# A transformer layer's opening, the start of its ConvFFN and the down projection's operands rearranged

## The chip, the cores and the metric

The kernel runs on one core of a Trainium2 chip, in one launch. The metric is the device time of the whole launch in microseconds. The core has five engines that work side by side and wait for each other through semaphores: TensorE (matrix products, into PSUM banks), VectorE, ScalarE, GpSimd (elementwise work; GpSimd doesn't touch PSUM) and SyncE, whose queue issues all of this kernel's DMAs.

## The reference

One layer of a diffusion backbone on 1024 tokens of width 1024, with 256 context tokens, all float32:

```
mod_x = silu(c) @ w_ada + b_ada              # six vectors: shift, scale, gate, twice
hx = rms_norm(x) * (1 + sc1) + sh1           # the context likewise, with its own c
...                                          # Fourier branch and gated DeltaNet branch on hx
x = x + gt1 * rms_norm(merged @ w_out)
h = rms_norm(x) * (1 + sc2) + sh2
a, u = split(h @ w_up)                       # two halves of 2816 channels
a = dwconv2d(a, conv_ffn)                    # 3x3 on the 16 x 64 grid of tokens
x = x + gt2 * rms_norm((silu(a) * u) @ w_down)
```

## The kernel before, in words

**Products in three parts.** Matrix products are made at float32's precision from faster float32r products: each operand is split into a high part (a copy to float32r) and a low part (the operand less the high part), and high x high, high x low and low x high are summed in a PSUM bank. So every operand costs one copy and one difference on ScalarE, VectorE or GpSimd. `halves` and `weights` load and split a weight tile, `split` an activation; a weight's low part overwrites its raw tile.

**The order of instructions.** The function `layer` records operations in a natural order. `Program.schedule` then orders them for each engine: it gives each operation a cost by a formula, ranks it by the longest path to the end plus a `bonus` that the code sets around urgent parts, and hands out ready operations by rank in a simulated time. What it decides is fixed in the program; on the chip each engine goes through its list in order. Tiles live in pools, stacked from the left or the right of SBUF; a tile that reuses the words of another, of its own ring or of a pool closed before, waits for the other's last reader. A PSUM bank is named by a tag ("X0", "Y0", "X1", "Y1", "pp", "pf", "pd", "pm"), one 128x512 tile each.

**The opening** (from `rows`, and `hidden_x`). The first 2048 columns of `w_ada`, shift and scale, are loaded in 16 tiles of 128x1024 (row block k, `half` 0 for the shift and 1 for the scale), split, and multiplied with `s4`, which holds the high and the low part of silu(c) for the tokens and the context in four columns. The four rows of 512 are then transposed and summed into `mod`. `hidden_x` normalizes x, transposes it in blocks of 512 tokens, applies `mod` on ScalarE and splits the result: the high part on VectorE, the low part on VectorE and GpSimd in turn. `decays` is the first product behind it.

**The output projection** (loop `for ts in ...`). For each tile of 128 tokens, 48 matmuls (`wo_group`: 8 row blocks k of the weights, three part products, two banks), then `post` (norm over the two banks and residual; squares on ScalarE, a power on GpSimd, the rest on VectorE), a store of the new residual to DRAM, a second norm, and scaling in place. Tokens 6 and 7 are done together. After four tiles (g = 0, and again g = 1) `transposed` and ScalarE make `hh[k, g]`, the modulated hidden tile, channel block k by 512 tokens.

**The ConvFFN.** The up projection is one level of a Strassen scheme: instead of eight products of half matrices there are seven per column block c of 128 channels (22 blocks). The right operands `RB[m]` are four tiles each, made once: `side_b` splits an `hh` tile, `sum_b` first adds or subtracts two. RB[1] and RB[3] need the first 512 tokens alone, RB[4] the second, RB[0], RB[2], RB[5] and RB[6] both. For each c, `both` loads four raw weight tiles; `summed` makes sums of them on GpSimd, `split_w` splits on ScalarE and GpSimd; `chain` is 12 matmuls into bank A, B or C. A block has seven chains, 84 matmuls, called here by the code's names m1 to m7, recorded as 2, 5, 1, 4, 3, 7, 6; between chains of one bank its result is evicted (to `v_`, `u_` or the padded grid `apad`). The 3x3 convolution follows: per half one ScalarE and eight VectorE operations in PSUM, then silu and the product with u, and a store to DRAM (`gdr`).

**The down projection.** Three groups of token tiles (3, 3 and 2); for each, the 22 blocks of the gated activation are loaded back, split (`down_g`, low part on GpSimd) and multiplied with `w_down`'s split blocks, most of which stay in SBUF.

## Time and profile before

| | |
|---|---|
| median of 3 runs | 2068.61 us (2061.31 to 2069.54) |
| the profiled execution | 2066.87 us |
| its span, first to last instruction | 2065.2 us |
| mean granted TensorE clock | 0.973 |
| TensorE, weight loads, VectorE, ScalarE, GpSimd busy | 94%, 76%, 65%, 41%, 32% |
| DMA | 257.5 MB, mean 125 GB/s |

The profile is one execution. Its page gives each engine's busy time, a map of 40 slices (each digit the busy share in tenths; PEclk the granted TensorE clock in tenths), the chain of work that ended last, and groups of instructions with count, busy time, mean duration and the idle time before them by what ended it. All operations are recorded by one helper, so every row has its line (L349); one tells them apart by engine, operation, operands (m is an SBUF tile, p a PSUM bank, d a DRAM tile), shape and time. PE is TensorE, PEld its weight loads, DVE VectorE, ACT ScalarE, POOL GpSimd, SPq the DMA queue. Besides the page, the answers for one stretch are used: busy times by stretch, the timeline of one engine, and the groups of a stretch.

### The profile page before, as it was taken

What the parts mean: (1) busy time and instruction counts of PE and PEld (TensorE: products, weight loads), DVE (VectorE), ACT (ScalarE), POOL (GpSimd) and SP (SyncE); (2) the same over time, 40 slices, a digit from 0 to 9 for tenths busy, and PEclk for the clock granted to TensorE, in tenths of its full rate; (3) what the DMA queues carried; (4) which work ended last, traced back from release to release, by engine and by line L of the source; (5) the groups of instructions that cost most, each with busy time, mean ns of one, the idle gap of its engine ahead of it and who ended that gap; (6) DMA issues with size and microseconds to landing.
All of it is one profiled execution on the core that took longest, in us unless ns stands there. A gap on an engine that the chain in (4) does not pass through costs nothing. (4 is left out here: it accounts for less than half of the span.)

```text
span 2065.2 us, 31554 instructions
## 1 busy us (share of the span) xinstructions
PE 1949.2 (94%) x11470; PEld 1573.0 (76%) x11470; DVE 1349.2 (65%) x2780; ACT 856.5 (41%) x2074; POOL 670.9 (32%) x671
## 2 busy tenths in 40 slices
PE   6988999899998999999999999949999999999998
PEld 2777878687787788778787778728788888887886
DVE  7647776768677677673756484477988888891021
ACT  6367345555354453533431132334444444541121
POOL 4210121201112220210211000387888888722222
PEclk9999999899998999999999999959999999999999
DMA  7143324344442543341778462302222222452231
GB/s 285 44 163 120 105 85 138 113 137 134 119 135 53 154 151 100 111 114 46 226 251 306 162 214 96 113 33 69 90 82 81 84 83 81 158 201 88 86 124 53
DMA packets 180637, 257.52 MB, mean 125 GB/s; under 512 B 75921, under 2 KB 97522, under 8 KB 180482
## 3 DMA queue, kind: packets, MB, share of 16 engines
q1 hardware_dynamic: 180482, 255.51, 38.6%
q8 instruction: 90, 1.47, 0.3%
q14 instruction: 65, 0.53, 0.1%
HBM read 194.52 MB, written 60.94 MB: 124 GB/s over the span
## 5 line engine op out<-in xcount | busy, mean ns | idle before, releaser
L349 PE MATMUL p<-m,m 128*128 128x512 f32 (+7 forms) x11310 | 1934.7, 338 | 98.5 <-ACT m L349 51.8
L349 PEld LDWEIGHTS p<-m,m 128*128 128x128 f32 (+4 forms) x11310 | 1554.1, 174 | 469.7 <-ACT m L349 77.3
L349 POOL TENSOR_TENSOR m<-m,m 128x512 fp32r<-128x512 f32 (+7 forms) x436 | 556.8, 1297 | 713.1 <-DVE m L349 382.9
L349 ACT ACTIVATE m<-m 128x512 fp32r<-128x512 f32 (+9 forms) x635 | 407.8, 656 | 623.7 <-DMA m<-d 152.0
L349 DVE TENSOR_TENSOR m<-m,m 128x512 f32<-128x512 f32 (+26 forms) x1006 | 528.2, 536 | 112.9 <-ACT m L349 87.3
L349 ACT ACTIVATE m<-p 128x512 f32<-128x512 f32 (+5 forms) x510 | 221.8, 447 | 325.5 <-PE p L349 283.1
L349 DVE SCALAR_TENSOR_TENSOR m<-p,m,m 128x128 f32<-128x128 f32 (+4 forms) x488 | 202.9, 451 | 89.9 <-ACT m L349 40.1
L349 DVE SCALAR_TENSOR_TENSOR p<-m,m,p 128x512 f32<-128x512 f32 x352 | 240.2, 750 | 3.0
L349 ACT ACTIVATE m<-p,m 128x128 f32<-128x128 f32 (+2 forms) x240 | 115.4, 491 | 194.8 <-PE p L349 181.5
L349 POOL MEMSET m<- 128x1024 f32 (+7 forms) x79 | 35.1, 456 | 369.3 <-PE p L349 223.6
L349 DVE SCALAR_TENSOR_TENSOR m<-m 128x1 f32<-128x1 f32 (+1 forms) x25 | 5.0, 199 | 197.3 <-ACT m L349 197.3
L349 POOL COPY m<-m 32x256 f32<-32x256 f32 (+2 forms) x136 | 60.6, 449 | 205.7 <-DMA m<-d 172.6
L349 DVE TENSOR_TENSOR m<-p,m 128x512 f32<-128x512 f32 (+4 forms) x91 | 57.9, 647 | 55.7 <-PE p L349 53.0
L349 DVE SCALAR_TENSOR_TENSOR m<-m,m 128x512 f32<-128x512 f32 (+5 forms) x119 | 66.7, 568 | 33.6 <-ACT m L349 21.2
L349 DVE COPY m<-p 32x256 f32<-32x256 f32 (+10 forms) x116 | 42.2, 368 | 65.3 <-PE p L349 34.6
L349 DVE TENSOR_TENSOR m<-m,p 128x128 f32<-128x128 f32 (+3 forms) x117 | 53.4, 459 | 28.3 <-PE p L349 27.1
L349 DVE SCALAR_TENSOR_TENSOR m<-m,m,m 128x1024 f32<-128x1024 f32 (+2 forms) x68 | 54.4, 801 | 19.3 <-DMA m<-in_w_ada_dram 18.8
L349 ACT ACTIVATE p<-p 128x128 f32<-128x128 f32 x208 | 55.0, 265 | 19.3 <-PE p L349 17.3
L349 DVE SCALAR_TENSOR_TENSOR m<-m,p 128x512 f32<-128x512 f32 x76 | 50.8, 682 | 15.4 <-PE p L349 10.6
L349 DVE SCALAR_TENSOR_TENSOR m<-m,m,p 128x128 f32<-128x128 f32 x128 | 42.7, 342 | 23.1 <-PE p L349 22.5
L349 ACT ACTIVATE m<-m,m 128x128 f32<-128x128 f32 (+1 forms) x168 | 54.5, 400 | 6.2 <-DMA m<-d 5.0
L349 POOL TENSOR_SCALAR_AFFINE_SELECT m<-m 128x1024 f32<-128x1024 f32 x16 | 18.8, 1191 | 100.1 <-DVE m L349 100.1
(20 smaller groups left out, 227.3 us busy)
## 6 DMA issues: line engine op xcount, KB each, us to landing
m<-d SPq DMA_DIRECT2D x76, 512.0 KB
d<-m SPq DMA_DIRECT2D x138, 256.0 KB
m<-d SPq DMA_DIRECT2D x114, 256.0 KB
m<-in_wi_dram SPq DMA_DIRECT2D x106, 256.0 KB
m<-in_w_ada_dram SPq DMA_DIRECT2D x48, 512.0 KB
m<-in_wu_dram SPq DMA_DIRECT2D x88, 256.0 KB
m<-in_wn_dram SPq DMA_DIRECT2D x26, 512.0 KB
m<-d SPq DMA_DIRECT2D x44, 192.0 KB
```

What stands on the lines that cost most here:

```text
L349: return getattr(engine.real, method)(*[real(v) for v in args], **{k_: real(v) for k_, v in kw.items()})
```

## The change

*Opening.* The shift half of `w_ada` is no longer split: eight tiles `whole`, multiplied as plain float32 with `s`, into rows of two; the scale half is split as before, its low parts on VectorE and GpSimd in turn. The modulated token tile takes three tags in turn instead of one. In `hidden_x` the high part goes to VectorE and ScalarE in turn, the low part always to VectorE. The weights of `decays` get tiles of their own.

*Start of the ConvFFN.* The tiles of the split output weights are laid out in pairs, k by k. Three pairs of banks take turns in the output projection; its last group is tokens 5, 6, 7: five row blocks for all three, then the last three for each. All sums and low parts of RB move to VectorE, all high parts to ScalarE. The tiles for u and v come ahead of RB's, which are 22; the last of RB[5] takes a free tile of two older pools. The seven chains of blocks 0 and 1 are recorded interleaved, those that need only the first tokens first; the convolution becomes a function of its own. The first tokens' `hh` and most evictions get a bonus.

*Down projection.* The low parts of the activation move from GpSimd to VectorE.

```diff
-WB = {"H": 8, "L": 8, "h": 3, "l": 3, "fh": 2, "fl": 3, "woh": 8, "wol": 8, "dh": 3, "dl": 3}
+WB = {"H": 8, "L": 8, "h": 3, "l": 3, "fh": 2, "fl": 3, "woh": 8, "wol": 8, "dh": 3, "dl": 3, "LT": 2, "tk": 2}
...
-    rows = [ps(t_, [4, HALF], f"modr{i}") for i, t_ in enumerate(("pd", "pm", "pp", FBANK))]
+    rows = [ps(t_, [(2, 4)[i // 2], HALF], f"modr{i}") for i, t_ in enumerate(("pd", "pm", "pp", FBANK))]
...
     for k in range(KT):
-        for half in range(2):
+        whole = hx.tile([P, D], F32, tag="LH"[k % 2], name=f"w_ada{k}0", bufs=KT)
+        sp.dma_start(whole, a["w_ada"][k * P:(k + 1) * P, 0:D])
+        for j in range(2):
+            te.matmul(rows[j], s[:, k, :], whole[:, j * HALF:(j + 1) * HALF], start=k == 0, stop=k == KT - 1)
+        for half in range(1, 2):
             parts = halves(a["w_ada"][k * P:(k + 1) * P, half * 1024:(half + 1) * 1024], hx, ("H", "L"),
-                           f"ada{k}{half}", (ve, po)[half * (k % 2)])
+                           f"ada{k}{half}", (ve, po)[k % 2])
             for j in range(2):
                 for i, w_ in enumerate(parts):
                     te.matmul(rows[half * 2 + j], s4[:, k, :], w_[:, j * HALF:(j + 1) * HALF], start=k + i == 0,
...
-        mr = dt("th", f"modrow{q}", (4, HALF))
+        n = (2, 4)[q // 2]
+        mr = dt("th", f"modrow{q}", (n, HALF))
         ve.tensor_copy(mr, rows[q])
         for j in range(4):
-            te.transpose(pm_[:, q * 4 + j, :], mr[:, j * P:(j + 1) * P], ident[0:4, 0:4])
+            te.transpose(pm_[:, q * 4 + j, 0:n], mr[:, j * P:(j + 1) * P], ident[0:n, 0:n])
...
-    ve.tensor_tensor(mod, mod, pm_[:, :, 2:4], op=ALU.add)
+    ve.tensor_tensor(mod[:, 8:16, :], mod[:, 8:16, :], pm_[:, 8:16, 2:4], op=ALU.add)
...
-                xt = dt("th", f"xm{k}{g}", (P, HALF))
+                xt = dt(("N", "N", "th")[k % 3], f"xm{k}{g}", (P, HALF))
                 se.activation(xt, pt, AF.Identity, scale=mod[:, 8 + k, 0:1], bias=mod[:, k, 0:1])
-                split(hH[k][:, hs], hL[k][:, hs], xt, ve, (ve, po)[k % 2])
...
-        wba = weights(a["wi"][0], "ba")
+        wba = weights(a["wi"][0], "ba", tags=("LT", "tk"), pl=dp)
...
     wop = pool("wo", bufs=1, side="right")
+    for _ in range(KT):
+        for t_ in ("woh", "wol"):
+            wop.tags.setdefault(t_, []).append(wop.region(D))
...
-        (ve.tensor_copy(h_, src) if n % 2 else se.activation(h_, src, AF.Copy))
-        (ve, po)[n % 2].tensor_tensor(l_, src, h_.bitcast(F32), op=ALU.subtract)
...
-        (ve, po)[(m + n) % 2].tensor_tensor(t_, x_, y_, op=op)
+        ve.tensor_tensor(t_, x_, y_, op=op)
...
-    wo_banks = [("X0", "Y0"), ("X1", "Y1")] * 3 + [("X0", "Y0"), ("pp", FBANK)]
+    wo_banks = [("X0", "Y0"), ("X1", "Y1"), ("pp", FBANK), ("X0", "Y0"), ("X1", "Y1"), ("pp", FBANK), ("X0", "Y0"),
+                ("X1", "Y1")]
...
-    for ts in ((0,), (1,), (2,), (3,), (4,), (5,), (6, 7)):
+    for ts in ((0,), (1,), (2,), (3,), (4,), (5, 6, 7)):
         pts, xts = {}, {}
+        early = 5 if len(ts) > 1 else 0
         for t in ts:
             xts[t] = wp.tile([P, D], F32, tag="xt", name=f"xr{t}", bufs=5)
             sp.dma_start(xts[t], a["x"][t * P:(t + 1) * P, :])
             pts[t] = [ps(wo_banks[t][g], [P, HALF], f"wo{t}{g}") for g in range(2)]
-        for k in range(KT):
+        for k in range(early):
             for t in ts:
                 wo_group(t, k, pts[t], 3 * k)
         for t in ts:
+            for k in range(early, KT):
+                wo_group(t, k, pts[t], 3 * k)
             xt = xts[t]
             post(pts[t], xt, g1r, f"o{t}", wp)
...
         g = ts[-1] // 4
+        prog.bonus = BON * (1 - g)
         for k in (0, 4, 1, 5, 2, 6, 3, 7) if g == 0 else (4, 5, 6, 7, 0, 1, 2, 3):
             pt = transposed(xn[-4:], k, f"h2{g}", ("pd", "pm")[k % 2])
...
+        prog.bonus = 0.0
...
     RAW, WH, WL = 8, 5, 5
-    h2p = pool("h2p", bufs=24, side="right")
+    upr = pool("upr", bufs=1, side="right")
+    for t_, n, m in (("v", 2, HALF), ("u", 3, T)):
+        upr.tags[t_] = [upr.region(m) for _ in range(n)]
+    h2p = pool("h2p", bufs=22, side="right")
...
     for i in range(4):
+        if i == 3:
+            rings[5] = (mp[0], mp[1])
         sum_b(5, hh[i, 0], hh[i, 1], ALU.add, i)
     close(hb)
-    upr = pool("upr", bufs=1, side="right")
...
+        def step(m):
+            if m == 2:
+                chain(A, summed("u0", "u1", ALU.add, "m2"), 1, True)
+                first(lambda: se.activation(v_, A, AF.Copy, scale=-1.0))
+            elif m == 5:
+                chain(B, summed("a0", "a1", ALU.add, "m5"), 4, True)
...
+                chain(A, split_w(raw["u1"], f"m4{c}", True), 3, False)
+                first(lambda: se.activation(u_[:, 0:HALF], A, AF.Copy))
...
+
+        def first(f):
+            prog.bonus = BON
+            f()
+            prog.bonus = 0.0
+
+        def last():
+            conv(c, ap_, inner, u_)
+        return step, last
...
+    pairs = [both(c) for c in range(2)]
+    for m, c in ((2, 0), (4, 0), (2, 1), (4, 1), (5, 0), (5, 1), (3, 0), (3, 1), (1, 0), (7, 0), (6, 0), (1, 1), (7, 1),
+                 (6, 1)):
+        pairs[c][0](m)
+        if m == 6:
+            pairs[c][1]()
+    for c in range(2, NC_FF):
+        step, last = both(c)
+        for m in (2, 5, 1, 4, 3, 7, 6):
+            step(m)
+        last()
+    for p_ in (h2p, upr, wq, lp[1], lp[0], mp[1], mp[0], upl):
         close(p_)
...
             gl = gst.over(gf, F32R, f"gl{c}_{blk}")[:, 0:width]
-            po.tensor_tensor(gl, gf, gh.bitcast(F32), op=ALU.subtract)
+            ve.tensor_tensor(gl, gf, gh.bitcast(F32), op=ALU.subtract)
```

The steps not shown (m = 1, 3, 5 and 7) wrap their chain and eviction in the same way; the evictions behind m7 and m6 have no bonus.

More of the change, by code (lines that the diff above doesn't have):

```diff
@@ L655, in hidden_x @@
                 pt = transposed(xs, k, f"x{g}", XY[k % 4])
-                xt = dt("th", f"xm{k}{g}", (P, HALF))
+                xt = dt(("N", "N", "th")[k % 3], f"xm{k}{g}", (P, HALF))
                 se.activation(xt, pt, AF.Identity, scale=mod[:, 8 + k, 0:1], bias=mod[:, k, 0:1])
-                split(hH[k][:, hs], hL[k][:, hs], xt, ve, (ve, po)[k % 2])
+                split(hH[k][:, hs], hL[k][:, hs], xt, (ve, se)[k % 2], ve)
     def hc(k):
@@ L1470, in side_b @@
         h_, l_ = m_tile(hp, f"bH{m}{n}"), m_tile(lp_, f"bL{m}{n}")
-        (ve.tensor_copy(h_, src) if n % 2 else se.activation(h_, src, AF.Copy))
-        (ve, po)[n % 2].tensor_tensor(l_, src, h_.bitcast(F32), op=ALU.subtract)
+        se.activation(h_, src, AF.Copy)
+        ve.tensor_tensor(l_, src, h_.bitcast(F32), op=ALU.subtract)
         RB.setdefault(m, []).append((h_, l_))
@@ L1584, in both, with conv @@
         grid = lambda t_: t_.rearrange("p (a b) -> p a b", b=GW)
-        chain(A, summed("u0", "u1", ALU.add, "m2"), 1, True)
-        se.activation(v_, A, AF.Copy, scale=-1.0)
-        chain(B, summed("a0", "a1", ALU.add, "m5"), 4, True)
-        ve.tensor_tensor(v_, v_, B, op=ALU.subtract)
-        chain(C, summed("a0", "u1", ALU.add, "m1"), 0, True)
-        ve.tensor_tensor(v_, v_, C, op=ALU.add)
-        chain(A, split_w(raw["u1"], f"m4{c}", True), 3, False)
-        se.activation(u_[:, 0:HALF], A, AF.Copy)
-        chain(B, split_w(raw["a0"], f"m3{c}", True), 2, False)
-        se.activation(inner(1), grid(B), AF.Copy)
-        chain(A, summed("a1", "u1", ALU.subtract, "m7"), 6, False)
-        ve.tensor_tensor(inner(0), grid(A), grid(v_), op=ALU.add)
-        chain(B, summed("u0", "a0", ALU.subtract, "m6"), 5, False)
-        ve.tensor_tensor(u_[:, HALF:T], B, v_, op=ALU.add)
+        def step(m):
[4 more added lines that the diff above has]
+                chain(B, summed("a0", "a1", ALU.add, "m5"), 4, True)
+                first(lambda: ve.tensor_tensor(v_, v_, B, op=ALU.subtract))
+            elif m == 1:
+                chain(C, summed("a0", "u1", ALU.add, "m1"), 0, True)
+                first(lambda: ve.tensor_tensor(v_, v_, C, op=ALU.add))
+            elif m == 4:
+                chain(A, split_w(raw["u1"], f"m4{c}", True), 3, False)
+                first(lambda: se.activation(u_[:, 0:HALF], A, AF.Copy))
+            elif m == 3:
+                chain(B, split_w(raw["a0"], f"m3{c}", True), 2, False)
+                first(lambda: se.activation(inner(1), grid(B), AF.Copy))
+            elif m == 7:
+                chain(A, summed("a1", "u1", ALU.subtract, "m7"), 6, False)
+                ve.tensor_tensor(inner(0), grid(A), grid(v_), op=ALU.add)
+            else:
+                chain(B, summed("u0", "a0", ALU.subtract, "m6"), 5, False)
+                ve.tensor_tensor(u_[:, HALF:T], B, v_, op=ALU.add)
+        def first(f):
[5 more added lines that the diff above has]
+        return step, last
+    def conv(c, ap_, inner, u_):
         for g in range(2):
@@ L1613, in both @@
             sp.dma_start(gdr[c, :, hs], th_)
-    for c in range(NC_FF):
-        both(c)
-    for p_ in (upr, h2p, wq, lp[1], lp[0], mp[1], mp[0], upl):
+    pairs = [both(c) for c in range(2)]
[10 more added lines that the diff above has]
+    for p_ in (h2p, upr, wq, lp[1], lp[0], mp[1], mp[0], upl):
         close(p_)
```

## The prediction

> **What bounds the kernel now.** I read the page's busy table and its forty slices first, then the busy times by stretch, then the engines' timelines around the two places that stand out.
>
> ```profile
> span 2065.2 us, 31554 instructions
> PE 1949.2 (94%) x11470; PEld 1573.0 (76%) x11470; DVE 1349.2 (65%) x2780; ACT 856.5 (41%) x2074; POOL 670.9 (32%) x671
> PE   6988999899998999999999999949999999999998
> PEclk9999999899998999999999999959999999999999
> ```
>
> TensorE bounds it: 94% busy, and every slice but a few is full. What a change can take away is TensorE's idle and half-clock time. There are two such places that the diff touches: the opening (first slices) and the valley of slice 27 between the output projection and the ConvFFN. Rows by stretch, columns: length, then PE, PEld, DVE, ACT, POOL busy, the granted clock, DMA share and GB/s.
>
> ```profile
> 29.00:39.50 10.50, 8.04 (x32) 2.91 (x30) 8.34 (x11) 6.37 (x10) 3.51 (x3) 0.72 1.03 407
> 43.00:58.60 15.60, 9.88 (x50) 6.64 (x48) 14.23 (x34) 13.08 (x24) 9.84 (x8) 0.83 0.00 1
> 1338.30:1391.80 53.50, 22.88 (x69) 14.03 (x69) 40.68 (x41) 19.03 (x33) 43.47 (x35) 0.62 0.09 32
> 1391.80:1396.00 4.20, 4.20 (x11) 3.33 (x12) 1.34 (x2) 0.00 (x0) 2.00 (x2) 0.56 0.00 0
> 1396.00:1427.00 31.00, 31.00 (x139) 25.63 (x138) 21.29 (x31) 14.14 (x23) 23.35 (x18) 1.00 0.19 58
> 1600.00:1700.00 100.00, 100.00 (x443) 82.84 (x442) 88.41 (x126) 43.59 (x74) 81.01 (x63) 1.00 0.24 82
> 1820.00:1840.00 20.00, 20.00 (x87) 16.01 (x86) 20.00 (x25) 8.02 (x12) 6.62 (x6) 1.00 0.37 124
> 1860.00:1900.00 40.00, 40.00 (x172) 32.04 (x171) 2.77 (x5) 6.26 (x15) 8.68 (x9) 1.00 0.15 43
> ```
>
> In the valley TensorE is busy 22.9 of 53.5 us, at 0.62 of its clock: about 14 us of work at full clock, so some 39 us are lost, and 2 more in the half-clock run-up behind it (4.2 us at 0.56). VectorE (40.7) and GpSimd (43.5) are the busy ones there. Before and behind it TensorE is full; in the down projection (1860 on) it is full with VectorE nearly idle.
>
> **The valley, now.** TensorE's timeline (start, length, engine, operation, count, idle before and releaser):
>
> ```profile
> 1329.67 7.20 PE L349 MATMUL p<-m,m 128*128 128x512 f32 x32
> 1337.53 0.73 PE L349 MATMUL p<-m,m 128*128 128x512 f32 x2 [0.66 <-ACT m L349]
> 1366.50 2.06 PE L349 MATMUL p<-m,m 128*128 128x512 f32 x3 [5.31 <-ACT m L349]
> 1387.50 1.22 PE L349 MATMUL p<-m,m 128*128 128x512 f32 x2 [9.81 <-ACT m L349]
> ```
>
> The output projection ends at 1336.9; call it W. The seven chains of column blocks 0 and 1 are 168 matmuls. Of the 69 instructions in the valley 32 are transposes of the second token half, 37 are chain matmuls; 11 follow by 1396; the other 120 run at 31.0/139 = 0.22 us (a few records may be missing) and end at 1422.4. So blocks 0 and 1 are through at W+85.5. I price the new valley as the time from W to that point.
>
> **The valley, changed.** Without any wait: 168 x 0.22 = 37.0, plus the 32 transposes (groups of the valley, the last three of the whole run; columns: count, busy us, mean ns, idle before and releasers):
>
> ```profile
> L349 PE MATMUL p<-m,m 128*128 128x128 f32 x32 | 7.6, 387 | 8.6 <-DVE m L349 5.5 <-ACT m L349 3.1
> L349 DVE TENSOR_TENSOR m<-m,m 128x512 f32<-128x512 f32 x11 | 15.8, 1443 | 2.0 <-POOL m L349 1.2 <-ACT m L349 0.5
> L349 DVE TENSOR_TENSOR m<-m,m 128x512 fp32r<-128x512 f32 x11 | 11.9, 1080 | 4.7 <-ACT m L349 4.7
> L349 DVE CAST m<-m 128x512 fp32r<-128x512 f32 x11 | 8.6, 782 | 4.9 <-ACT m L349 2.5 <-POOL m L349 2.3
> ...
> L349 ACT ACTIVATE m<-m 128x512 fp32r<-128x512 f32 x330 | 205.7, 628 | 379.7 <-POOL m L349 138.5 <-DVE m L349 77.8 <-PE p L349 67.9
> L349 ACT ACTIVATE m<-p,m 128x512 f32<-128x512 f32 x80 | 56.4, 719 | 94.1 <-PE p L349 82.2 <-DVE m L349 8.3 <-POOL m L349 3.4
> L349 DVE TENSOR_TENSOR m<-p,m 128x512 f32<-128x512 f32 x80 | 54.5, 686 | 55.7 <-PE p L349 53.0 <-ACT m L349 2.5
> ```
>
> 7.6 x 0.62 = 4.7 us at full clock. The floor is 41.7, and with two waits for an eviction between chains of one bank (about 1 us each) W+44. Step by step:
>
> Chains 2 and 4 of both blocks need only the first token half. The ordering by hand puts them first, and the output weights now lie k by k, so that the ConvFFN's raw weights fall on k = 0, 1 and their split parts on k = 2 to 4, which the last group (three token tiles, five k's first) finishes 54 matmuls, 11.9 us, before W. Of GpSimd's 24 sums and differences for the two blocks the eight for the first five chains then fit ahead of W+1, and four more follow as chains give up their buffers. The third tile of that group takes the banks that tile 4 has just left; its first product may wait for tile 4's norm, but the other tiles' products stand ready: nothing (0 to 2). So TensorE does four chains, 10.6 us plus the two waits, to W+12.6, where it now waits.
>
> The last token tile must pass its norm meanwhile. For tile 4, with engines free, that took from the first square to the end of the scaling:
>
> ```profile
> 1316.02 0.60 ACT L349 ACTIVATE m<-p 128x512 f32<-128x512 f32 x1 [5.22 <-PE p L349]
> 1323.91 0.76 DVE L349 TENSOR_SCALAR m<-m,m 128x1024 f32<-128x1024 f32 x1 [2.16 <-DMA d<-m]
> 1319.46 1.28 DVE L349 TENSOR_TENSOR m<-m,m 128x512 f32<-128x512 f32 x2
> 1360.25 2.92 DVE L349 TENSOR_TENSOR m<-m,m 128x512 fp32r<-128x512 f32 x2 [0.47 <-ACT m L349]
> 1332.65 14.29 POOL L349 TENSOR_TENSOR m<-m,m 128x512 f32<-128x512 f32 x11 [0.40 <-PE p L349]
> 1391.62 1.09 POOL L349 TENSOR_TENSOR m<-m,m 128x512 fp32r<-128x512 f32 x1 [1.14 <-DVE m L349]
> ```
>
> 8.7 us; I take W+9.5. Tiles 5 and 6 end 8 and 4 us before W now and are hidden. Then come the operands from the second half: 4 differences and 16 sums with 16 differences, all on VectorE: 36 operations. Alone VectorE takes 0.64 (1319.46), beside a busy GpSimd 1.46 (1360.25) or, by the two groups above, (15.8 + 11.9)/22 = 1.26. The two take turns, so I add both: 36 x 0.64 = 23.0, GpSimd's remaining 12 operations for the blocks at 1.09 = 13.1, three for block 2 = 3.3, and 3 of the 5.5 us of VectorE's eight evictions (0.69) that I guess don't overlap: 42.4, so the last operand stands at W+52. The 11 casts (8.6 us) go to ScalarE, which has 20 copies at 0.63 and 8 evictions at 0.72 there: 18 us, hidden behind VectorE's. Chains 5, 3, 1 and 7 are done by then; the last, chain 6 of block 1, ends 3.5 us later: **W+55.5**, a gain of 30. The Trainium skill, page "SBUF — State Buffer", section "Who interferes with whom", says that a VectorE operation with two SBUF inputs and a reading GpSimd one exclude each other for a whole instruction, and the loser waits. By that rule the sum is the one just made from the rows; the plain mean of 1.26 is the rival below.
>
> Costs of the same edit: the convolutions of blocks 0 and 1 queue behind that VectorE work. VectorE has 88.4 of 100 us in the steady stage, so it wins back 2 us a block of 18.5 us (84 x 0.22); I take 2 us of TensorE waits (0 to 8). The last operand tile of chain 6 now lies where the down projection's second weight block is loaded, so that load waits for the ConvFFN's very last chain: 1 us (0 to 4), since the first weight block covers 18 x 0.22 = 4 us. Raising evictions in rank: nothing (-1 to 3), TensorE being full there.
>
> **The opening.** Now:
>
> ```profile
> L349 PE MATMUL p<-m,m 128*4 128x512 f32 x64 | 20.9, 478 | 14.5 <-ACT m L349 9.2 <-DVE m L349 5.2
> L349 PE MATMUL p<-m,m 128*1 128x512 f32 x16 | 8.2, 590 | 0.0
> L349 POOL TENSOR_TENSOR m<-m,m 128x1024 fp32r<-128x1024 f32 x8 | 20.0, 2504 | 78.7 <-DVE m L349 39.7 <-PE p L349 14.0 <-DMA m<-in_wo_dram 12.6
> 6.28 1.06 ACT L349 ACTIVATE m<-m 128x1024 fp32r<-128x1024 f32 x1 [3.64 <-DMA m<-in_w_ada_dram]
> 28.64 2.27 ACT L349 ACTIVATE m<-m 128x1024 fp32r<-128x1024 f32 x2 [0.22 <-DMA m<-in_w_ada_dram]
> 34.93 1.20 DVE L349 TENSOR_TENSOR m<-m,m 128x1024 fp32r<-128x1024 f32 x1
> 33.30 6.13 PE L349 MATMUL p<-m,m 128*4 128x512 f32 x22 [2.17 <-DVE m L349]
> 42.50 0.24 DVE L349 SCALAR_TENSOR_TENSOR m<-m,m 128x8 f32<-128x8 f32 x2
> ```
>
> The last modulation weights are in by 30.9, but a late low part (to 36.1) holds the products to 39.4, and the modulation is ready at 42.7. Changed, half of the weights need no split: ScalarE loses 8 and VectorE 8 of the 1024-wide operations. The last low part is GpSimd's (2.5 us, behind a copy that ends near 30): done near 32.5. TensorE's load grows: a plain product is two instructions of 8.2/16 = 0.51 us, 32 of them 16.4, plus 32 split ones at 20.9/64 = 0.33, 10.5: 27 us from the first landing near 6.3, so about 34. That is 5.4 before today. Behind it VectorE gives up 8 casts and takes 8 differences of the main tokens, about even; the decay weights in tiles of their own and four buffers more for the modulated tokens only let work start earlier, nothing to 1. I take **5 us**; 9 if the products keep up with the landings, -8 if half of the 27 us run at half clock (13 us more).
>
> **The down projection.** TensorE enters it without a gap:
>
> ```profile
> 1797.79 32.40 PE L349 MATMUL p<-m,m 128*128 128x512 f32 x138 [0.71 <-POOL m L349]
> ```
>
> 66 differences (22 in each of three groups of token tiles) leave GpSimd. From 1860 on VectorE has 2.8 of 40 us busy: nothing gained or lost. At 1820 it is full with the last convolutions, and 22 more operations of some 0.5 us (an estimate, 0.64 for three quarters of the width) delay these by 11 us; their result is wanted three blocks before the first group's end, near 1798 + 19 x 18 x 0.22 = 1873, when they are over by 1860 now: nothing, or up to 5 if that cover is short.
>
> **Sum**, against the profiled execution's 2066.9 us (span 2065.2; the runs' median is 2068.6, so 2 above it): 30 - 2 - 1 + 5 = 32, **2035 us**.
>
> **Rivals.**
> 1. *VectorE keeps up*: operands are never late, the valley ends at W+44 and the opening gives its 5: 41 + 5 - 1 = 45, **2022**. For it: ScalarE and VectorE have little to do before W. Against: 36 operations in the 31 us from W+9.5 to 3.5 before the end is 0.86 each, below the mean of 1.26.
> 2. *Contention at the mean*: 36 x 1.26 + 5.5 = 51 from W+9.5, end at W+64; with 6 us of convolution backlog 21 - 6 - 1 + 5 = 19, **2048**. For it: these are this stretch's own durations.
> 3. *The early chains don't come early*: the program's list scheduler or SyncE's queue puts the weights behind the stores of the normed tokens, TensorE stands till W+12 and does them later; 10.6 less of the 30, **2046**.
> 4. *Half clock*: the paced stretch keeps TensorE at 0.5, as 1338 to 1391 nearly did: ten chains at 5.3 and the transposes at twice 4.7 end at W+75; 10.5 - 2 - 1 + 5, **2054**. The Trainium skill, "TensorE: Matmul & The Clock Gate", "HAM oscillation — how this bites in real kernels", says that idle gaps beyond some 3.4 us bring the half rate back. Against: TensorE would be 60% busy there, and 43 to 58.6, as busy, had 0.83.
> 5. *Slower*: VectorE becomes the bound of the whole ConvFFN. It now needs 16.4 us a block; if the new order of evictions and waits on GpSimd lifts that above TensorE's 18.5, each of twenty blocks pays the excess. From 20.1 us a block the gain is gone; at 20.7, 20 x 2.2 = 44 - 32: **2079**. For it only that VectorE takes over work; against, none of that work recurs per block.
>
> **How the numbers follow.** Forecast 0.50, rivals in order 0.18, 0.14, 0.08, 0.06, 0.04. Range 2015 (rival 1 with the opening's 9 us) to 2054 (rival 4), which leaves out rival 5 and the forecast's worse ends. A measurement of this kernel can tell about 0.5%, 10 us, from no change: only rival 5 is slower (0.04); rival 4 and the tails of 2 and 3 give 0.03 within it; 0.93 faster.
>
> **What would show it.** Right: TensorE over 60% busy in the 50 us behind the output projection with transposes among chains, GpSimd's share below, chain 6 last; the modulation near 37 us; VectorE's 384-wide differences in the down projection with TensorE full. Wrong: a TensorE gap over 10 us behind the output projection; VectorE over 95% busy at steady ConvFFN with TensorE below 1; products of the opening ending at 39 or later; TensorE gaps in 1800 to 1860.

## The result and the profile after

Changed, the kernel takes 2052.0 us (median of 7 runs, 2047.95 to 2056.52) where it took 2065.6 (median of 7, 2061.3 to 2069.5): 0.9936 of the time before, 95% interval 0.9918 to 0.9954. It is faster, by 13.5 us where 32 were forecast. The profiled execution took 2047.95, the fastest of the seven; beside the profiled one before it is 19 us shorter.

The page of after, its busy times and three of its rows by slice:

```profile
span 2046.2 us, 31495 instructions
PE 1953.0 (95%) x11470; PEld 1570.9 (77%) x11470; DVE 1363.1 (67%) x2848; ACT 858.1 (42%) x2088; POOL 564.0 (28%) x573
PE   8989999899999999999999999979999999999998
DVE  5648767667677577673655485479988889882132
PEclk9989999899999999999999999999999999999999
```

The half-clock slice of the valley is gone. VectorE has two slices of 9 in a row, 1381 to 1483, at the valley's end and behind it. The same views by stretch as in the prediction, now of after (length, then PE, PEld, DVE, ACT, POOL busy, clock, DMA share, GB/s):

```profile
43.00:58.60 15.60, 14.49 (x85) 11.16 (x84) 14.59 (x35) 15.52 (x28) 4.22 (x4) 0.98 0.00 1
1330.40:1383.90 53.50, 41.27 (x164) 28.96 (x163) 40.60 (x45) 26.77 (x51) 31.32 (x24) 0.94 0.16 54
1400.00:1420.00 20.00, 17.37 (x77) 14.05 (x76) 19.86 (x31) 8.92 (x16) 15.57 (x13) 1.00 0.24 83
1480.00:1500.00 20.00, 16.27 (x59) 12.78 (x58) 15.81 (x24) 7.81 (x14) 13.29 (x11) 0.83 0.18 64
1600.00:1700.00 100.00, 100.00 (x443) 82.81 (x442) 90.48 (x125) 42.61 (x73) 83.64 (x64) 1.00 0.25 85
```

In the 53.5 us behind the output projection (its last matmul, by the program's order, ends at W = 1330.4) TensorE is busy 41.3 instead of 22.9, at 0.94 of its clock instead of 0.62, on 164 instructions instead of 69. The opening's row has 85 TensorE instructions for 50. The steady stage is full as before. New are losses at 1400 and 1480. The first is this wait of TensorE (groups of instructions in order of time: start, length, engine, operation, count, idle before and releaser):

```profile
1403.22 22.07 PE L349 MATMUL p<-m,m 128*128 128x512 f32 x96 [2.63 <-ACT m L349]
```

By the program's order it waits for ScalarE's copy of a weight sum of block 3 that GpSimd has just made; the bank of the chain behind it is freed 0.3 us later, by a VectorE eviction (at 1402.87) behind the convolution of block 0.

Both kernels issue 11,470 matmuls, so their starts can be set side by side by count: the start of the n-th one in a kernel less that in the kernel before. The differences of these differences say where time came from (us, minus is gained). All traces of the study are in one table; each is one execution.

| kernel, its profiled time | to matmul 400, opening | 400 to 8400, attention | 8400 to 9000, valley | 9000 to 9200, block 5 | 9200 to 10600, entry to the down projection |
|---|---|---|---|---|---|
| after, 2048 | -11.9 | +4.5 | -21.5 | +6.9 | +3.0 |
| after_again, 2045 | -11.6 | -0.9 | -18.9 | +6.6 | +3.0 |
| after_third, 2051 | -11.5 | +6.8 | -21.7 | +6.9 | +3.0 |
| e1_open, 2060 | -11.2 | +7.9 | -3.4 | 0.0 | +0.3 |
| e11_open_mod, 2064 | -3.1 | +2.9 | -3.1 | 0.0 | 0.0 |
| e2_ffn, 2047 | +0.4 | 0.0 | -20.0 | +0.2 | -0.4 |
| e2_again, 2046 | +0.1 | -0.2 | -20.1 | +0.1 | -0.4 |
| e2_third, 2058 | +0.1 | +2.9 | -23.2 | +0.2 | +10.5 |
| e4_gl_ve, 2063 | +0.8 | -1.0 | -2.7 | 0.0 | -0.9 |
| e3_gl_po, 2036 | -11.8 | +1.7 | -20.4 | +0.2 | -0.4 |
| e3_again, 2053 | -11.5 | +5.0 | -18.7 | +0.2 | +10.6 |
| e3_third, 2045 | -11.5 | +0.8 | -22.5 | +0.2 | +11.1 |
| e5_quiet, 2038 | -11.5 | +5.3 | -29.9 | +5.4 | +3.4 |
| e6_late, 2050 | -11.5 | +7.0 | -18.7 | +6.6 | -0.8 |
| e7_first4, 2043 | -11.8 | +3.8 | -19.2 | +0.2 | +3.0 |
| e7_again, 2047 | -11.2 | +6.4 | -19.0 | +0.2 | +3.4 |
| e8_wve, 2044 | -10.9 | +4.5 | -23.9 | +3.9 | +3.0 |
| e10_f4late, 2041 | -11.8 | +4.5 | -18.7 | +0.2 | -0.1 |
| e9_comb, 2040 | -10.9 | +8.2 | -23.6 | 0.0 | -0.8 |

The opening gave twice its forecast, the valley two thirds, and two losses that had been priced at 2 and 1 took 10. (Three kernels with the old ConvFFN run the valley 3 us shorter than the one profiled execution of before, so some 3 of every number in that column are that execution's own. In after, the wait at 1400 takes 2.9 back in the same column, between matmuls 8750 and 8800.) The attention part is 4.7 longer than before on average in the 14 traces with the opening's whole edit, and 0.9 in the five others; why is not shown.

### The profile page after: what moved, and what is told of

The parts are those of the page before. It is cut to its first block, busy times and chain, and to the rows that moved or that the text cites. A ratio compares the mean times of both kernels' runs of the same rounds, so it can differ in the third digit from the quotient of the medians.

```text
span 2046.2 us, 31495 instructions
## 1 busy us (share of the span) xinstructions
PE 1953.0 (95%) x11470; PEld 1570.9 (77%) x11470; DVE 1363.1 (67%) x2848; ACT 858.1 (42%) x2088; POOL 564.0 (28%) x573
## 4 chain that ended last, share of the span: by engine, by line
PE 71%; DVE 14%; DMA 5%; ACT 5%; issue 2%; POOL 1%; SPq 0%; DVEq 0%; POOLq 0%; ACTq 0%
PE p L349 71%; DVE m L349 11%; ACT m L349 4%; DMA m<-d 3%; DVE p L349 3%; DMA d<-m 2%; ACT p L349 1%; POOL m L349 1%; DMA m<-in_w_ada_dram 1%; SPq L349 0%; DMA m<-in_wu_dram 0%; ACT L349 0%; DVEq L1787 0%; POOLq L1787 0%; DVEq L349 0%
## 5 line engine op out<-in xcount | busy, mean ns | idle before, releaser
L349 DVE TENSOR_TENSOR m<-m,m 128x512 fp32r<-128x512 f32 (+27 forms) x1096 | 557.4, 523 | 253.4 <-ACT m L349 222.8
L349 ACT ACTIVATE m<-m 128x512 fp32r<-128x512 f32 (+8 forms) x649 | 411.3, 652 | 613.5 <-DMA m<-d 161.0
L349 POOL TENSOR_TENSOR m<-m,m 128x512 fp32r<-128x512 f32 (+5 forms) x338 | 449.5, 1353 | 782.6 <-DVE m L349 625.1
L349 DVE COPY m<-p 32x256 f32<-32x256 f32 (+11 forms) x116 | 42.1, 368 | 62.5 <-PE p L349 32.8
L349 DVE SCALAR_TENSOR_TENSOR m<-m,m,m 128x1024 f32<-128x1024 f32 (+2 forms) x68 | 59.6, 878 | 26.0 <-DMA m<-in_w_ada_dram 25.6
L349 ACT ACTIVATE p<-p 128x128 f32<-128x128 f32 x208 | 55.4, 266 | 25.6 <-PE p L349 23.6
L349 DVE SCALAR_TENSOR_TENSOR m<-m,m,p 128x128 f32<-128x128 f32 x128 | 42.7, 342 | 23.5 <-PE p L349 22.8
L349 POOL TENSOR_SCALAR_AFFINE_SELECT m<-m 128x1024 f32<-128x1024 f32 x16 | 18.9, 1199 | 100.4 <-DVE m L349 100.4
```

The lines of the kernel that those rows point to most:

```text
L349: return getattr(engine.real, method)(*[real(v) for v in args], **{k_: real(v) for k_, v in kw.items()})
```

## The experiments

### Each part alone

The diff taken apart: the opening's edits alone; the ConvFFN's alone, with the low parts `gl` of the down projection left on GpSimd; the whole without its third part; the third part alone. (The experiments ran on several chips, each beside runs of the kernel before, whose medians agree: 2065.6 to 2066.7.)

```diff
 # e3_gl_po, on the changed kernel (e4_gl_ve is the reverse, on the kernel before)
-            ve.tensor_tensor(gl, gf, gh.bitcast(F32), op=ALU.subtract)
+            po.tensor_tensor(gl, gf, gh.bitcast(F32), op=ALU.subtract)
```

> The opening's part of the change alone, on the kernel before. Theory from the two traces: the modulation comes 4 us earlier and VectorE and ScalarE are so much freer behind it that matmul 200 starts 10 to 11 us earlier than before; 0 to 3.5 us of it are lost again in the attention part; 7 to 11 us faster than before. Rival, the forecast's own price: 5 us faster, all of it the earlier modulation. Second rival: the 11 us exist only with the rest of the change (another order of the planner): under 3 us.

> The ConvFFN's part alone, on the kernel before; the down projection's low parts stay on GpSimd. Theory: the valley gains 20 us (36 operand operations on VectorE from about W+19 to W+58), about 3 of it go back to the stall behind block 5 and 3 to the load of the down projection's second weight tile; 13 to 16 us faster. Rival, the forecast's sizes: 30 - 2 - 1 = 27 us faster.

> The change without its third part: the down projection's low parts are GpSimd's again. Theory: three of these low parts (1.65 us each on VectorE, beside GpSimd) ran in the middle of the ConvFFN ahead of a convolution that TensorE waited for, and brought the 3.7 us gap and the half clock behind it; without them 3 to 5 us faster than the change as a whole. Rival, the forecast's price: 0 (within 1.5 us), the stall stays where it was. Second rival: GpSimd is then late at the end of the ConvFFN: 1 to 3 us slower.

> The third part alone, on the kernel before. Theory: VectorE has 88 of 100 us busy there and no backlog from the valley, so three low parts of 1.6 us are absorbed: 0 (within 1.5 us of before). Rival: VectorE is late whatever the valley does: 2 to 5 us slower. Second rival: the down projection's entry gains from a freer GpSimd: 1 to 2 us faster.

Measured against the same runs of the kernel before (median 2065.6): e1 2054.7, ratio 0.9953 (0.9937 to 0.9968); e2 2059.4, 0.9965 (0.9948 to 0.9982); e3 2051.4, 0.9920 (0.9893 to 0.9947); e4 2064.7, 0.9992 (0.9978 to 1.0006). So the opening alone is worth 11, and the third part alone nothing, as the theory had it. The other two answer in two ways: their profiled executions are as the theory said or better (2047, 2036), their medians 12 and 15 us above these. By its median e3 is no faster than the whole change. Something in them comes and goes.

### What comes and goes: a starved low part

Kernels were profiled again without any edit. "The planner" in what follows is `Program.schedule`.

> The changed kernel once more, for a second profiled execution. Theory: executions differ by what TensorE's clock does where it is paced by others (the first profiled one, 2048, was the fastest of its seven; median 2052); a slower one will show a granted clock below 0.9 over some stretch of 10 to 20 us in the attention part or in the valley behind the output projection, and the same gaps otherwise. Rival: the executions differ by gaps (VectorE and GpSimd in another order of turns), at the same clock.

> The kernel of e3_gl_po once more: its profiled execution took 2036 and its median is 2051. Theory: an execution at the median loses its 15 us as half clock in stretches where TensorE is paced (valley or attention), since the mean granted clock of such runs is 0.976 to 0.981 against 0.984. Rival: by gaps of TensorE at the same clock.

> The ConvFFN's part alone once more: its profiled execution took 2047 and its median was 2059. Theory: in an execution near the median one low part on GpSimd lasts 8 to 20 us at the down projection's start, while VectorE runs its differences without a pause, and TensorE stands 8 to 12 us there. Rival: the 12 us lie in half clock in the valley or the attention part, and the low parts take 1 to 2 us each.

> The ConvFFN's part alone a third time. Theory: if this execution takes over 2055, one low part on GpSimd lasts 8 to 20 us at the down projection's start with TensorE standing; if it takes 2047, none does. Rival: over 2055 without such a low part, by half clock or gaps elsewhere.

> The changed kernel without its third part a third time. Theory: over 2045 only with one low part on GpSimd lasting 8 to 20 us at the down projection's start; about 2037 to 2042 without. Rival: the time differs by half clock in the attention part or the valley alone.

after_again took 2045.1, e3_again 2052.7, e2_again 2046.5, e2_third 2057.5, e3_third 2044.8. The second execution of e3 lost 10.6 us more than the first in one place, the entry into the down projection. Of GpSimd, VectorE and TensorE there (start, length, engine, operation, count, idle before and releaser), in e3_again:

```profile
1802.54 1.55 POOL L349 TENSOR_TENSOR m<-m,m 128x384 fp32r<-128x384 f32 x1 [3.00 <-ACT m L349]
1804.39 23.13 POOL L349 TENSOR_TENSOR m<-m,m 128x384 fp32r<-128x384 f32 x4 [0.29 <-ACT m L349]
...
1804.32 19.45 DVE L349 TENSOR_TENSOR m<-m,m 128x512 f32<-128x512 f32 x18
...
1824.68 10.56 PE L349 MATMUL p<-m,m 128*128 128x512 f32 x36 [8.83 <-POOL m L349]
```

and in the first execution of the same program, e3_gl_po:

```profile
1799.26 1.49 POOL L349 TENSOR_TENSOR m<-m,m 128x384 fp32r<-128x384 f32 x1 [0.30 <-ACT m L349]
1803.30 1.15 POOL L349 TENSOR_TENSOR m<-m,m 128x384 fp32r<-128x384 f32 x1 [2.55 <-ACT m L349]
...
1799.20 24.41 DVE L349 TENSOR_TENSOR m<-m,m 128x512 f32<-128x512 f32 x18
```

At the entry VectorE runs 18 operations in a row with two inputs each from SBUF: the ConvFFN's last two products, then 16 low parts of weights (128x1024, 1.22 us each where nothing holds them up). In the first execution GpSimd's low parts get their turns among them, and the row of VectorE is 5 us longer for it. In the second, one low part that began 0.07 us after VectorE's row ends only after it: four operations take 23.13, of which three need 1.0 each, so the first took 20. TensorE, which needs it, stands 8.83 us and then runs at half clock (0.53 in 1824.7 to 1829). e2_third shows the same, 23.14 for four operations and a gap of 8.83; e3_third 22.76 and 9.90. e2_again, at 2046, has none over 2.1 us, and its TensorE runs through. So of six traces of the two kernels with `gl` on GpSimd beside the new ConvFFN three have it, at +10.5 to +11.1 us each, and the three others lose nothing there. So for e3_again the theory of half clock fell: of the 16.5 us between it and the first execution 11.0 are this place. The rest is the attention part (3.3) and the valley (1.7). e3_third lost as much here and still took 2044.8, so the time alone doesn't tell.

The third part of the change takes this away: in none of the eleven traces with `gl` on VectorE at the entry does it occur (the longest GpSimd operation in them is 5.2 us). Before the change the last convolutions, which read PSUM, still lay among VectorE's differences there, and in its trace GpSimd gets every turn.

### What the third part costs

The first four of these low parts have buffers from the start, so the planner runs them in the middle of the ConvFFN. VectorE's and TensorE's rows at block 5 of after; the first is a summary of one stretch, with shortest, median and longest ns:

```profile
L349 DVE TENSOR_TENSOR m<-m,m x4: 1639/1646/1785, 1471.8 to 1476.7; 128x384 fp32r<-128x384 f32 x3, 128x512 f32<-128x512 f32 x1
...
1470.84 7.47 DVE L349 TENSOR_TENSOR m<-m,m 128x512 f32<-128x512 f32 x5
1479.03 8.79 DVE L349 SCALAR_TENSOR_TENSOR p<-m,m,p 128x512 f32<-128x512 f32 x13
1487.73 0.68 DVE L349 TENSOR_TENSOR m<-m,p 128x512 f32<-128x512 f32 x1
...
1479.75 5.06 PE L349 MATMUL p<-m,m 128*128 128x512 f32 x21
1488.55 11.65 PE L349 MATMUL p<-m,m 128*128 128x512 f32 x38 [3.73 <-DVE m L349]
```

Three low parts of 1.64 us (1.02 on GpSimd in the trace of before; the fourth operation of that summary, of 512 columns, is a product) delay 13 operations of a convolution, these delay the eviction at 1487.73, and TensorE waits 3.73 us for it. The 38 matmuls behind that take 11.65 us where 38 x 0.226 (100/443 in the steady stage) are 8.6: half clock, another 3. The Trainium skill, page "TensorE: Matmul & The Clock Gate", section "HAM oscillation — how this bites in real kernels", has an idle gap of that length bring the half rate; this trace agrees (0.83 in 1480 to 1500, 0.50 in 1488.5 to 1493).

```diff
 # e7_first4
-            ve.tensor_tensor(gl, gf, gh.bitcast(F32), op=ALU.subtract)
+            (po if blk == 0 and c < 4 else ve).tensor_tensor(gl, gf, gh.bitcast(F32), op=ALU.subtract)
 # e6_late: where the down projection's weight tiles lie
     wn = pool("wn", bufs=1, side="right")
+    for at in (0, 5, 2, 6, 4, 1, 3, *range(7, NRES)):
+        for t_ in "hl":
+            wn.tags[f"{t_}{at}"] = [wn.region(D)]
 # e10_f4late: both
```

> The changed kernel with the down projection's weight tiles 1 and 5, and 3 and 6, in each other's place, so that no early weight block lies over the last operand of the ConvFFN's last chain. Theory: the wait of 2.0 us for the second weight block, and 1 to 1.5 us behind it, go: 2 to 3.5 us faster. Rival: the wait moves to VectorE's low parts of the weights amid the last convolutions: 0 to 1 us.

> The changed kernel with only the first four low parts of the down projection's first group back on GpSimd (these are the ones that the planner runs in the middle of the ConvFFN); the other 62 stay on VectorE. Theory: the stall behind block 5 (6.6 us in each of four traces of kernels with the third part, 0 in the two without it) goes, and GpSimd's low parts, which waited up to 20 us behind VectorE's 18 differences in a row at the down projection's start in the second execution of the kernel without the third part, can't: 5 to 10 us faster than the changed kernel, with a spread of its runs under 8 us. Rival: the stall comes from the convolutions' backlog alone and stays: 0 to 2 us.

> The first four low parts on GpSimd as in e7_first4, and the down projection's weight tiles in changed places as in e6_late. Theory: the two are separate losses, 6.6 and 3.5 us by the traces: 8 to 10 us faster than the changed kernel, 2039 to 2044. Rival: without the stall the planner puts the ConvFFN's last chains in another order and the second loss isn't there in the first place (as in the kernel without the third part): no faster than e7_first4.

e6 took 2049.0 (0.9910, 0.9894 to 0.9926), 3 us less than the changed kernel; e7 2045.2 (0.9905, 0.9886 to 0.9924), 7 less; e10 2038.7 (0.9871, 0.9853 to 0.9889), 13 less, with a spread of 5.6 us. e6 and e7 gain what their theories said, e10 more; the runs of e7 spread over 9.6 us, not under 8, so the stall was not all that made them differ. The stall behind block 5 is gone in both traces of e7 and in e10's, the loss at the entry in e6 and e10. TensorE at block 5 of e7_first4, and then at the entry of after and of e10_f4late:

```profile
1469.71 30.67 PE L349 MATMUL p<-m,m 128*128 128x512 f32 x134
```

```profile
1779.13 11.62 PE L349 MATMUL p<-m,m 128*128 128x512 f32 x49 [0.17 <-POOL m L349]
1792.73 1.69 PE L349 MATMUL p<-m,m 128*128 128x512 f32 x6 [1.99 <-ACT m L349]
1794.62 4.52 PE L349 MATMUL p<-m,m 128*128 128x512 f32 x18 [0.20 <-DVE m L349]
1799.65 15.55 PE L349 MATMUL p<-m,m 128*128 128x512 f32 x65 [0.51 <-DVE m L349]
```

```profile
1769.83 9.68 PE L349 MATMUL p<-m,m 128*128 128x512 f32 x42
1779.97 35.25 PE L349 MATMUL p<-m,m 128*128 128x512 f32 x149 [0.46 <-ACT m L349]
```

The wait of 1.99 is for the head of the second weight block, whose tile lies over the last operand of chain 6; 0.17, 0.20 and 0.51 come on top, 2.9 in all. It was absent in e3 without any such edit, since the planner there put chain 6 ahead of another chain. What is left open by e6 and e7 is why the two edits bring 13 together and 10 one by one; the medians' own spread (e7: 2040.8 to 2050.4) allows either.

> The changed kernel a third time. Theory: if it takes over 2050, the entry into the down projection costs more than the 3.5 us of the first two traces (5 to 10), since the weights for it are loaded late and their low parts then meet the last convolutions. Rival: the entry costs 3.5 us again and the difference lies in half clock in the attention part (matmuls 2400 to 8400).

> e7_first4 a second time; the first took 2043 with 3.6 us lost at the entry. Theory: if it takes over 2047, the entry costs 5 to 10 us. Rival: the entry costs 3.6 us again and the difference lies in the attention part.

after_third took 2051.3 and e7_again 2046.7, with +3.0 and +3.4 at the entry. For after_third the theory falls and the rival holds; e7_again stayed just under its 2047 and decides nothing. after_again, at 2045.1, was no slower execution either, so its theory was not tested. What differs most between executions of one kernel here is the attention part, -0.9 to +6.8 us over three executions of the changed one. Of after_again and after_third the same work in that part, 251 and 252 TensorE instructions:

```profile
819.00:823.00 4.00, 2.71 (x51) 1.63 (x51) 2.35 (x5) 2.27 (x4) 3.80 (x6) 1.00 0.99 267
823.00:832.00 9.00, 8.16 (x200) 6.53 (x186) 5.45 (x11) 7.59 (x31) 5.86 (x12) 1.00 0.46 155
```

```profile
822.00:826.50 4.50, 2.15 (x38) 1.16 (x40) 2.86 (x5) 1.93 (x4) 3.45 (x6) 1.00 0.80 214
826.50:839.00 12.50, 10.03 (x214) 8.13 (x200) 5.49 (x11) 8.05 (x31) 5.39 (x12) 0.86 0.43 128
```

13 us in the one, 17 in the other, which waits longer for a load (2.4 us, not 1.3) and for VectorE (2.1, not 0.5), and then runs at 0.86.

### The valley

```diff
 # e5_quiet, column blocks 0 and 1 only (quiet is c < 2)
-            po.tensor_tensor(s_, raw[x_], raw[y_], op=op)
+            po.memset(s_, 0.01)
...
-        po.tensor_tensor(l_, src, h_.bitcast(F32), op=ALU.subtract)
+        po.memset(l_.bitcast(F32), 0.0)
```

> GpSimd's sums and low parts of the raw weights of column blocks 0 and 1 are replaced by fills that read nothing (the values of these weights are left out, the matmuls stay). Theory (VectorE and GpSimd take turns): VectorE's 36 operand operations take 0.68 each, the last norm is ready at W+9.5 or sooner, the last operand stands near W+44 instead of W+58, and the kernel is about 10 us faster than the changed one. Rival: ScalarE's copies and evictions or the waits between engines pace the valley; under 3 us. Second rival: the clock eats the gain, TensorE now waiting longer at the start; 0 with a granted clock below 0.8 in the valley.

e5 leaves out the sums and low parts of the weights of two column blocks. It took 2039.1 (0.9867, 0.9852 to 0.9882), 13 less than the changed kernel, and its valley gains 29.9 where the changed kernel's three gain 18.9 to 21.7. VectorE in the valley of after, then of e5_quiet:

```profile
1342.11 0.75 DVE L349 TENSOR_SCALAR m<-m,m 128x1024 f32<-128x1024 f32 x1 [1.84 <-DMA d<-m]
1349.62 0.69 DVE L349 TENSOR_TENSOR m<-m,m 128x512 fp32r<-128x512 f32 x1 [6.75 <-ACT m L349]
1350.96 11.68 DVE L349 TENSOR_TENSOR m<-m,m 128x512 f32<-128x512 f32 x15 [0.65 <-ACT m L349]
...
1365.94 9.37 DVE L349 TENSOR_TENSOR m<-m,m 128x512 f32<-128x512 f32 x7
1375.23 0.67 DVE L349 TENSOR_TENSOR m<-m,p 128x512 f32<-128x512 f32 x1
1375.83 10.98 DVE L349 TENSOR_TENSOR m<-m,m 128x512 fp32r<-128x512 f32 x11
...
1387.32 1.19 DVE L349 TENSOR_TENSOR m<-m,m 128x512 fp32r<-128x512 f32 x1
```

```profile
1339.74 0.75 DVE L349 TENSOR_SCALAR m<-m,m 128x1024 f32<-128x1024 f32 x1 [1.71 <-POOL m L349]
1348.03 10.25 DVE L349 TENSOR_TENSOR m<-m,m 128x512 fp32r<-128x512 f32 x16 [7.53 <-ACT m L349]
1358.79 0.68 DVE L349 TENSOR_TENSOR m<-m,m 128x512 f32<-128x512 f32 x1
1360.09 3.94 DVE L349 TENSOR_TENSOR m<-m,m 128x512 f32<-128x512 f32 x6
1364.55 4.49 DVE L349 TENSOR_TENSOR m<-m,m 128x512 fp32r<-128x512 f32 x7
1369.72 5.26 DVE L349 TENSOR_TENSOR m<-m,m 128x512 fp32r<-128x512 f32 x4 [0.68 <-ACT m L349]
```

An operation takes 10.25/16 = 0.64 in e5, and 9.37/7 = 1.34 and 10.98/11 = 1.00 in after. GpSimd still issues as many instructions in e5; they only write, and they are shorter (0.53 us for a fill). The last row of e5 shows that the reads matter: there GpSimd works on the weights of block 2, which it still reads, and four operations of VectorE take 5.26/4 = 1.3 each. The Trainium skill, "SBUF — State Buffer", section "Who interferes with whom", makes just that difference, and these runs agree with it (0.64 beside the fills). The theory held: the last norm is ready at W+9.0 and the last operand at W+45.

```diff
 # e8_wve: blocks 0 and 1 but for chain m2's sums and m4's low part; e9_comb: e8 and e10
-            po.tensor_tensor(s_, raw[x_], raw[y_], op=op)
+            eng = ve if c < 2 and name != "m2" else po
+            eng.tensor_tensor(s_, raw[x_], raw[y_], op=op)
...
```

The lines not shown give `split_w` the same engine for the low parts.

> The changed kernel with the sums, differences and low parts of the raw weights of column blocks 0 and 1 on VectorE, but for those of their first two chains (m2, m4): 18 operations. Theory (the engines take turns): each cost VectorE 1.09 us of waiting and now costs 0.64 of its own time: the valley is 5 to 8 us shorter, of which the backlog of convolutions takes none. Rival: VectorE is the bound of the valley in its own right, and 18 x 0.64 = 11.5 us come on top of its 36 operations, while GpSimd's turns had cost it less: 2 to 6 us slower.

> e10_f4late and e8_wve together: first four low parts on GpSimd, weight tiles in changed places, and 18 of GpSimd's 24 weight operations for blocks 0 and 1 on VectorE. Theory: the losses are separate and add up: 4 to 6 us faster than e10_f4late's 2038.7, so 2033 to 2035. Rival: VectorE, which takes 18 operations more ahead of the convolutions, is later behind block 5 again and gives it back: within 2 us of e10_f4late.

e8 took 2045.3 (0.9910, 0.9892 to 0.9928), e9 2039.2 (0.9862, 0.9843 to 0.9881). The valley of both is 2 to 5 us shorter than the changed kernel's (23.9 and 23.6), and e8 is 7 us faster than it by the medians; 3 of these lie behind block 5, where its trace loses 3.9 instead of 6.6 to 6.9. On top of e10 it brings nothing that four and five runs can tell (2039.2 to 2038.7): here the rival holds for the time, though not for its reason, since e9 loses nothing behind block 5; its one trace loses 8.2 in the attention part. e10_f4late and e9_comb are the fastest versions that do all the work, some 27 us under the kernel before.

### The opening

e11_open_mod is e1_open without these two lines:

```diff
-                xt = dt("th", f"xm{k}{g}", (P, HALF))
+                xt = dt(("N", "N", "th")[k % 3], f"xm{k}{g}", (P, HALF))
-                split(hH[k][:, hs], hL[k][:, hs], xt, ve, (ve, po)[k % 2])
+                split(hH[k][:, hs], hL[k][:, hs], xt, (ve, se)[k % 2], ve)
```

> The opening's part alone on the kernel before, without its edits to the main tokens' copies (three buffers instead of the two, casts on VectorE and ScalarE by turns and all low parts on VectorE are left as before). Theory: the modulation is 4 us earlier as before, and the other 7 us of the opening's 11 came from these copies: 3.5 to 5 us faster than the kernel before. Rival: the freer engines behind the plain products give the whole of it, and the copies' edits nothing: 9 to 11 us faster.

It took 2063.0 (0.9986, 0.9976 to 0.9996): 3 us faster than the kernel before, where e1 is 11. The rival (9 to 11) falls; the theory's 3.5 to 5 is narrowly missed. So 3 belong to the rest of the opening's edits, the plain products above all, and 8 to the two lines. Groups of 40 to 70 us, of e11_open_mod and of e1_open (count, busy us, mean ns, idle before and releasers):

```profile
L349 POOL TENSOR_TENSOR m<-m,m 128x512 fp32r<-128x512 f32 x7 | 12.4, 1779 | 13.7 <-DVE m L349 13.7
L349 DVE TENSOR_TENSOR m<-m,m 128x512 fp32r<-128x512 f32 x12 | 10.1, 862 | 0.1
L349 ACT ACTIVATE m<-p,m 128x512 f32<-128x512 f32 x14 | 10.6, 774 | 8.5 <-DVE m L349 4.3 <-POOL m L349 3.3 <-PE p L349 0.9
```

```profile
L349 DVE TENSOR_TENSOR m<-m,m 128x512 fp32r<-128x512 f32 x21 | 13.6, 683 | 0.3 <-ACT m L349 0.2
L349 ACT ACTIVATE m<-p,m 128x512 f32<-128x512 f32 x16 | 11.7, 790 | 0.0
```

Every second low part was GpSimd's, at 1.78 us on average, with VectorE's at 0.86; now all are VectorE's at 0.68. ScalarE, which writes the modulated tiles, waited 8.5 us for operations of VectorE and GpSimd that still read the two buffers, and waits for nothing in e1. Shorter low parts and a third buffer both shorten that wait. The two lines weren't tried one without the other, and the second also moves half of the casts to ScalarE, so how much is whose stays open.

## Why the prediction was right or wrong

**The valley, 30: the mechanism right, the size wrong.** The early chains ran early, the clock stayed up (0.94), VectorE's differences set the end, and it came at about W+65 (by the program's order blocks 0 and 1 end at W+68.6, with 4 us of block 2 done among them) instead of W+55.5. The step that failed is "Then come the operands from the second half", put right behind the norm at W+9.5. The norm ended at W+12.5, held up by GpSimd's weight operations. Then VectorE stood 6.75 us, since transposes and ScalarE's copies lie between the norm and the first difference; no term held that step. VectorE began the first operand at W+19.3, 9.8 late. The 36 operations and four evictions from there took 38.9 us, 3.5 under the 42.4 forecast for them: pricing them as turns, own time plus GpSimd's, came close. Behind the last operand it took 6.4 us and not 3.5, since chain 6 of block 0 waited for it too. These three make the 9 us. e5 shows what the turns cost: without them the last norm is ready at 1340.5, W+9.0 there (W = 1331.5), and the valley gains 30. Rival 2 named the right time, W+64, by luck: it took 1.26 us for an operation, where (38.9 - 4 x 0.68)/36 = 1.0 was measured, and the excess stood in for the missing step. Its 2048, which is also the profiled time, owes as much to an opening of 11 where it had 5.

**The backlog of convolutions, 2 (0 to 8): 7.** Within its bounds, but not by the convolutions alone: e7 takes the loss to 0.2 by moving four low parts and no convolution, and the third part alone (e4) loses nothing there, so it takes both. The 2.9 of the wait at 1400 come on top; whether they are the convolutions' or GpSimd's is not separated, and with them the bound is passed.

**The third part, "nothing gained or lost": wrong twice, in opposite directions.** The forecast looked for its cost where the low parts are used, from 1860 on and at 1820, and not where the planner runs the first four of them, in the middle of the stage where VectorE is the late one: the same 7. And it did not see that it takes away a starvation of 11 us that the rest of the change brings on in half of the traces. By the medians the two cancel (e3 2051.4, the whole 2052.0).

**The load behind chain 6, 1 (0 to 4): 3**, inside its bounds. e6 shows it to be the tile's place.

**The opening, 5: 11.** The products were priced rightly. In the first row below TensorE has done 48 of the 64 product instructions by 28; the other 16 lie among the transposes of the next row, as the groups of 28 to 36 show, and the last one ends at 34.6, where 34 was forecast. The modulation's first half is ready at 38.6 instead of 42.7, and e11 gives this part 3. What failed are two terms next to each other: "VectorE gives up 8 casts and takes 8 differences of the main tokens, about even", and the buffers that "only let work start earlier, nothing to 1". Together they brought 8 (e1 against e11). Counted in VectorE's operations the first is even; counted in turns with GpSimd, and by ScalarE's 8.5 us of waiting for its buffers, the two are not. Which of them brought how much is not shown.

```profile
7.78 20.06 PE L349 MATMUL p<-m,m 128*2 128x512 f32 x56 [7.78 <-DMA m<-in_w_ada_dram]
28.04 8.08 PE L349 MATMUL p<-m,m 128*128 128x128 f32 x36 [0.19 <-DVE m L349]
L349 PE MATMUL p<-m,m 128*2 128x512 f32 x8 | 3.6, 592 | 0.0
L349 PE MATMUL p<-m,m 128*4 128x512 f32 x8 | 2.2, 401 | 0.0
```

**The rivals.** Rival 1 fell with the first operand at W+19; 3 with the early chains; 4 with the clock. Rival 5's mechanism, VectorE late in the ConvFFN, happened for one block and not for twenty: VectorE has 90.5 of 100 us in the steady stage.

**The signs named beforehand** as wrong did not show: no TensorE gap over 1.9 us in the valley, VectorE at 90.5 in the steady stage, the opening's products over at 34.6, no TensorE gap in 1800 to 1860. They looked at the places that had been priced, and the losses of 3, 7 and 3 us lay at 1400, 1480 and 1790, which no sign covered.

The sum by the table for the profiled pair: -11.9 + 4.5 - 21.5 + 6.9 + 3.0 = -19.0. The median says -13.5: the profiled execution of the changed kernel lies 4 us under its median, that of the kernel before 1.3 over its own. The executions of the changed kernel spread over 11 us, of which the attention part, for which the forecast had no term, was seen to make 7.

## What to carry to other kernels

Where VectorE and GpSimd both read SBUF, count their operations as turns in one queue: moving work from GpSimd to the busier VectorE can gain (a valley 2 to 5 us shorter in e8; a part, not separated, of the 8 us in the opening), and a long row of two-input VectorE operations should have no GpSimd operation behind it that anyone needs soon. When an edit moves work to another engine, find where a planner will run each of the moved operations, not where they are used. And if a median lies far above a profiled execution, profile the same program again before explaining either.

## What the runs showed that was not expected

GpSimd does not always get its turn between two VectorE operations. In three of six traces one difference that takes 1.0 us alone waited through 18 VectorE operations, some 20 us; in the three others the same program's GpSimd operations took 1.0 to 2.1 us there. What decides it was not found: in e3_again the starved operation began 0.07 us behind VectorE's row, in e3_gl_po the row began 0.06 us ahead of one that was served after 1.49.
